# A two-layer decoder trunk (differential attention, then RWKV-7) on one NeuronCore: LoRA products begun with half of the tokens, states ahead of T's rows, T's loads between the masks

## The chip, the cores and the metric

The kernel runs on one core of one Trainium2 chip. The metric is the device time of one execution in microseconds, the median of several runs. TensorE multiplies matrices (PE in the profile, PEld for its weight loads), VectorE (DVE), ScalarE (ACT) and GpSimd (POOL) work element by element, SyncE (SP) issues most DMAs. Each engine takes its instructions in the order in which the program lists them for that engine.

## The reference

The trunk has two residual layers on 512 tokens of width 2048, all in float32. The first is gated differential attention, the second gated RWKV-7 time mixing:

```python
def rwkv7_mixer(h, ...):
    p = h @ w_in                                  # r, k, v, gate: 4 x 2048; dw, da: 96 each
    p = p + (token_shift(p) - p) * mu
    w_log = -softplus(-(w0 + tanh(dw) @ decay_up)) - 0.5
    decay = exp(-exp(w_log))
    a = sigmoid(a0 + da @ iclr_up)
    kk = heads(k * k_k);  kk = kk / max(norm(kk), 1e-12)
    k = k * (1.0 + (a - 1.0) * k_a)
    y = wkv7_scan(rh, heads(decay), kh, vh, -kk, kk * ah)   # S <- S*w + (S a) b' + v k';  y = S r
    y = group_norm(y) + sum(rh * kh * r_k) * vh
    return (y * silu(g)) @ w_out

for i in range(2):
    x = x + mixer_i(rms_norm(x, norm_w[i]))
```

There are 32 heads of 64 channels in the second layer; the scan runs over 512 tokens with a 64 x 64 state for each head.

## The kernel before

**Products.** Every large product is made of three matmuls on a high and a low part of both factors (`mm3`, L110 to 118), 16 channel tiles k of 128 for one sum. A weight is loaded on SP's queue (`wraw`), its high part is cast on ACT (`wh`, L102), its low part is the difference on DVE (`wl`, L103). Activations are split in the same way: `hH` on ACT, `hL` on DVE.

**Chains and ticks.** Work of another pair of heads runs between the matmuls of a projection. A `Chain` is a generator of steps, each of which yields the number of matmuls until the next. Every matmul of `mm3` that has the context counts as a tick of the oldest chain (`tick`); when its count is up, the next step is issued behind that matmul. If that step left a state (`g.state`), one item of `g.later`, elementwise work of the next pair, is issued behind it. What is still in `g.later` is issued by `stage2`. Priorities (`AHEAD`, `SCAN`, `SOLVE`) let a scheduler put instructions earlier in an engine's order; a larger one goes first.

**Between the layers.** The last columns of the first layer's output projection leave x, 4 blocks of 512 columns by 4 tiles of 128 tokens, in `xs`. `store_x` writes such a tile to memory and sums its squares (`junkx`, L727). The second layer's RMS norm then needs a reciprocal root for two token tiles at a time and a multiplication of each x tile by it (`scale`, L770): tokens 0 to 255 first, 256 to 511 last. `more_h` (L782 to 797) transposes a channel tile of all four token tiles into one PSUM bank (`xT`, L790) and splits it with `make_h` (L811, 812). The first products of the second layer are the LoRA down projections of decay and learning rate (192 columns in two sums of 96, `lora`), through `unit_chan` with `more_h`.

**The second layer's loop** goes over 16 pairs of heads, j. A pair's stages are spread over several rounds. Round j does, on PE: `stage2(j)` (makes `AR`, L1005, from the receptances), the V projection of j, `begin(j+1)` (K projection, and `stage1`, which puts `decays`, `queries`, `keys` of j+1 into `g.later`), the gate projection of j − 2 and the R projection of j + 1. Behind the 18th matmul of the V projection the function `behind` ends the chain of j − 2, issues `gram(j)`, `t_solve(j)` and `group_norm(j − 2)`.

- `gram` multiplies keys by queries in chunks of 64 tokens into PSUM (`gp`, L1021; first half with tag "pb", second half with tag "pc", two buffers each). With j > 1 it takes one step of the chain of j − 1 behind that. Then ACT copies to `G`, POOL writes the parts that T needs to memory (`ltd`) and masks G of head 0 and of head 1 (L1046, L1048).
- `t_solve` loads them again as `LT` (POOL's queue, L1071), inverts the triangles T row by row on DVE (`tmpl` L1082, `Tm` L1084, 31 rows; last L1085), and writes them to memory (`td`, L1086).
- The chain of j (`t_combine`, then `scan_pair`) loads `TT` from `td` on SP's queue (L1098), transposes it on DVE (`T1`, in the trace `T<-TT`, L1106), waits GAP_D ticks, multiplies with G (`px`, L1112), copies the result to `X` and a row of queries (`AR`) into G on ACT, waits GAP_X ticks, multiplies by TT (`px`, L1122). Then come eight chunks of the scan: `sm` (L1193) to `rhs`, `sm` (L1204) to `VS`, `sm` (L1211) to the next state `VS` on DVE (L1215, L1218), with copies of the state on POOL (`SA`, L1199) that are scaled by the decay (`Sg`, L1202). At the end `outputs` writes `Y` (L1233, L1237) into two PSUM banks of tag "pc", and `centre` subtracts the heads' means on DVE (`yc`, L1248 to 1250).
- `group_norm`, `finish_y` and `gated` make the rows of `yd2` in memory.

**The end.** After the loop the gates of the last pairs are projected; `gated(..., True)` splits the last two rows into high and low parts, `split_rows` the earlier ones as they come back from memory (`hH<-yr`, L421), and the output projection follows.

Of the kernel before, what the change touches and what calls it, by code (L numbers as in the profile page):

```python
# [13 lines left out]
F32 = mybir.dt.float32  # L14
# [4 lines left out]
ALU = mybir.AluOpType  # L19
# [16 lines left out]
    pass  # L36


AHEAD, SCAN, SOLVE = 2000, 3000, 4000


def ahead(offset):
# [549 lines left out]
def layer0(g, aps):  # L592
# [86 lines left out]
    with ExitStack() as cx:  # L679
# [42 lines left out]

        def store_x(cb, t):
            xr = xs[cb][:, t, :]
            nc.scalar.dma_start(out=g.xd[t * P : (t + 1) * P, cb * 512 : cb * 512 + 512], in_=xr)
            junk = g.work.tile([P, 512], F32, name="junkx", tag="a", bufs=2)
            nc.scalar.activation(junk[:], xr, AF.Square, accum_out=g.ssx[:, t, cb : cb + 1])  # L727

        sums = []
        one = lambda *tags: [(g.const if t[:2] == "dd" else g.work, t,  # L730
# [51 lines left out]
        def more_h(n, m):  # L782
            for k in range(len(g.hH), min(n, KT)):
# [7 lines left out]
                with tc.high_priority(offset=AHEAD):  # L791
                    make_h(g, ps, KT + k)

        pts = [g.ps.tile([P, 512], F32, name="lora", tag=tag) for tag in ("pb", "pc")]
        unit_chan(g, [(aps["rw_w_in"][0], 4 * D, 2 * RK)], 2 * RK, RK, more_h, pts=pts)
        g.dwda = []
        for i in range(2):
            m = shift_mix(g, pts[i], RK, g.mut[:, i : i + 1], g.omut[:, i : i + 1], "t1", 4)
# [3 lines left out]
    lx.close()  # L802


def make_h(g, ps, col):

    nc = g.nc
    hh = g.hp.tile([P, T], F32R, name="hH", tag="hH")
    hl = g.hp.tile([P, T], F32R, name="hL", tag="hL")
    w = g.prm_a[:, col : col + 1]  # L810
    m = nc.scalar.activation(hh[:], ps[:], AF.Copy, scale=w)  # L811
    d = nc.vector.scalar_tensor_tensor(hl[:], ps[:], w, hh[:].bitcast(F32), ALU.mult, ALU.subtract)
    g.hH.append(hh)
    g.hL.append(hl)
    return m.ins, d.ins


# [126 lines left out]
def stage1(g, j, k, up):  # L944
# [24 lines left out]
    def decays():  # L969
        nc.vector.tensor_tensor_scan(l[:].rearrange("p c t -> p (c t)"), g.rmask[:].rearrange("p c t -> p (c t)"),  # L970
                                     lw[:], 0.0, ALU.mult, ALU.add)
        nc.vector.tensor_scalar(m[:], l[:, :, C - 1], 0.5, None, ALU.mult)
        nc.vector.tensor_sub(l[:], l[:], m[:, :, None].to_broadcast([P, NC_, C]))
        nc.scalar.activation(p.E[:, :, 0], m[:], AF.Exp, scale=-1.0)
        nc.scalar.activation(p.E[:, :, 1:], l[:], AF.Exp)
        nc.scalar.activation(l[:], l[:], AF.Exp, scale=-1.0)
        nc.scalar.activation(p.f[:], tha[:], AF.Identity, bias=col("omka"), scale=col("hka"))
# [14 lines left out]
        nc.vector.tensor_add(p.gam[:, 0 : NC_ - 1], m[:, 0 : NC_ - 1], m[:, 1:NC_])  # L992
        nc.scalar.activation(p.gam[:, 0 : NC_ - 1], p.gam[:, 0 : NC_ - 1], AF.Exp)

    g.later += [decays, queries, keys]
    return p


# [11 lines left out]
def gram(g, j, p, before):  # L1010
# [30 lines left out]
                out=g.ltd[j % 2, half, h, :, 0:HALF].rearrange("c s t -> s c t"),  # L1041
                in_=p.G[q0 : q0 + HALF, :, 0, h, half * HALF : (half + 1) * HALF])

    for h in range(2):
        r_ = slice(h * C, h * C + C)
        nc.gpsimd.affine_select(out=p.G[r_, :, 0, 1 - h, :], in_=p.G[r_, :, 0, 1 - h, :], compare_op=ALU.is_ge,  # L1046
                                fill=0.0, base=-1, pattern=[[0, NC_], [1, C]], channel_multiplier=-1)
        nc.gpsimd.affine_select(out=p.G[r_, :, 1], in_=p.G[r_, :, 1], compare_op=ALU.is_ge, fill=0.0, base=0,  # L1048
                                pattern=[[0, NC_], [0, 2], [1, C]], channel_multiplier=-1)
# [11 lines left out]
@ahead(SOLVE)  # L1061
def t_solve(g, j, p):


    nc, w = g.nc, g.work
    NQ = HALF // NG
    LT = w.tile([P, HALF + 1, HALF], F32, name="LT", tag="LT", bufs=1)
    Tm = w.tile([P, NQ, HALF], F32, name="Tm", tag="Tm", bufs=1)
    tmp = w.tile([P, NQ * HALF], F32, name="tmpl", tag="tmpl", bufs=1)
    for i in range(NG):  # L1070
        nc.gpsimd.dma_start(out=LT[i * 32 : i * 32 + 32], in_=g.ltd[j % 2].rearrange("b h c s t -> (b h c) s t"))  # L1071
    n2 = LT[:, HALF, :]
    nc.vector.tensor_scalar(n2, n2, 1e-24, None, ALU.max)
# [11 lines left out]
    nc.vector.tensor_mul(Tm[:], Tm[:], n2[:, None, :].to_broadcast([P, NQ, HALF]))  # L1085
    nc.gpsimd.dma_start(out=g.td[j % 2].rearrange("q l t -> l q t"), in_=Tm[:])  # L1086


GAP_D, GAP_X, GAP_T = 18, 19, 8


def t_combine(g, j, p):
# [58 lines left out]
            nc.scalar.copy(p.VS[(1 - h) * C : (2 - h) * C, par : NC_ : 2, h, :], pv[par * C : par * C + C, :, h, :])  # L1151


def gate(g, j, gps):
    nc, w = g.nc, g.work
    gt = shift_mix(g, gps, P, *mus(g, 3, j), "v", 1)
    th = w.tile([P, T], F32, name="thg", tag="thg", bufs=1)
    nc.scalar.activation(th[:], gt[:], AF.Tanh, scale=0.5)
    nc.vector.scalar_tensor_tensor(gt[:], th[:], 1.0, gt[:], ALU.add, ALU.mult)
    return gt  # L1160


def gated(g, j, p, gt, last=False):
    g.nc.vector.tensor_mul(gt[:], gt[:], p.y[:])
    if last:
        return split_row(g, gt[:])
    g.nc.scalar.dma_start(out=g.yd2[j * P : (j + 1) * P, :], in_=gt[:])


# [12 lines left out]
def scan_pair(g, j, p, gap, gap_s, others):  # L1182
# [8 lines left out]
    for c in range(NC_):  # L1191
# [19 lines left out]
        nc.tensor.matmul(sm[:, o : o + P], p.BKT[:, c, :], both(VS[:, c]), start=True, stop=True)  # L1211
        for h, r_ in HEADS:
            s_ = sm[r_, o + h * C : o + h * C + C]
            if c:
                g.state = nc.vector.scalar_tensor_tensor(VS[r_, c + 1, h, :], s_, p.gam[r_, c : c + 1], Sg[r_, :],  # L1215
                                                         ALU.mult, ALU.add)
            else:
                nc.vector.tensor_scalar(VS[r_, c + 1, h, :], s_, p.gam[r_, c : c + 1], None, ALU.mult)  # L1218
        if c in others:
            others[c]()  # L1220
        yield gap_s
# [54 lines left out]
def layer1(g, aps):  # L1276
    nc, tc = g.nc, g.tc
    with ExitStack() as cx:
# [23 lines left out]
        for j in range(D // P):  # L1302
# [13 lines left out]
            def behind(m, j=j, p=p):  # L1316
                if j > 1:
                    pairs[j - 2].chain.finish(g)
                with tc.issue_after(m.ins):
                    gram(g, j, p, j > 1 and pairs[j - 1].chain)  # L1320
                t_solve(g, j, p)
                if j > 1:
                    group_norm(g, j - 2, pairs[j - 2])

# [131 lines left out]
```

## Time and profile before

| | us |
|---|---|
| median of 3 runs (lowest, highest) | 2209.49 (2206.18, 2210.26) |
| profiled execution, its own time | 2213.33 |
| its span | 2211.6 |
| PE busy | 2173.2 |
| DVE busy | 1445.7 |
| ACT busy | 1040.9 |
| POOL busy | 359.8 |

The span is the time from the profile's first instruction to its last. Times are us from its start, unless marked ns. In the views, a row gives engine, line, operation and tile names, `out<-in`; a bracket at the end gives how long the engine stood idle before the instruction and what it waited for. The granted clock is 1.00 at full speed. The first layer ends at 978.3 us, the loop over the pairs runs to about 2026 us, and the rest is the output projection.

### The profile page before, as it was taken

How to read it: one execution, taken by the hardware profiler on the slowest of the kernel's cores; microseconds unless marked ns; L12 is line 12 of the kernel's file. 1: busy time of each engine (PE TensorE's matmuls, PEld its weight loads, DVE VectorE, ACT ScalarE, POOL GpSimd, SP SyncE). 2: the span in 40 equal slices, each digit the busy share in tenths (PEclk: the TensorE clock that was granted, in tenths of full speed). 3: DMA queues.
4: the chain of work that ended last, by engine and by line, in shares of the span. 5: the costliest groups of instructions: out<-in, count | busy, mean ns of one | idle time of the engine just before them, and what ended most of it. 6: DMA issues, size and time to landing. Idle time of an engine off the chain costs nothing. (4 is left out here: it accounts for less than half of the span.)

```text
span 2211.6 us, 33922 instructions
## 1 busy us (share of the span) xinstructions
PE 2173.2 (98%) x12202; PEld 1762.5 (80%) x12202; DVE 1445.7 (65%) x3772; ACT 1040.9 (47%) x2110; POOL 359.8 (16%) x733
## 2 busy tenths in 40 slices
PE   9999999999999999989999999999999999999999
PEld 7888888888888878867777777778777777777887
DVE  5664646455564666465677788677777777777645
ACT  6443434344343454335455555555555556545322
POOL 0000000000000000110233233333332233331001
PEclk9999999999999999999999999999999999999999
DMA  6322232222222356643422333333333332345456
GB/s 192 97 85 97 77 102 89 87 95 86 96 86 95 129 183 213 162 106 90 106 67 78 79 92 86 82 91 94 98 91 82 89 88 75 107 131 182 174 166 120
DMA packets 281401, 240.21 MB, mean 109 GB/s; under 512 B 31792, under 2 KB 239744, under 8 KB 281232
## 3 DMA queue, kind: packets, MB, share of 16 engines
q1 hardware_dynamic: 256912, 190.13, 28.5%
q0 software_dynamic: 15456, 31.90, 6.7%
q10 hardware_dynamic: 8864, 16.01, 2.0%
q8 instruction: 96, 1.57, 0.3%
q14 instruction: 73, 0.60, 0.1%
HBM read 217.98 MB, written 19.99 MB: 108 GB/s over the span
## 5 line engine op out<-in xcount | busy, mean ns | idle before, releaser
L103 DVE TENSOR_TENSOR wl<-wraw,wh 128x1024 fp32r<-128x1024 f32 (+2 forms) x319 | 388.8, 1219 | 360.9 <-ACT wh L102 353.9
L102 ACT CAST wh<-wraw 128x1024 fp32r<-128x1024 f32 (+2 forms) x319 | 333.4, 1045 | 535.3 <-PE pp L114 374.5
L114 PE MATMUL pp<-wh,hH 128*128 128x512 f32 x1268 | 499.8, 394 | 4.0 <-ACT hH L421 2.4
L114 PE MATMUL pp<-wl,hH 128*128 128x512 f32 x1268 | 498.0, 393 | 0.0
L114 PE MATMUL pp<-wh,hL 128*128 128x512 f32 x1268 | 497.7, 393 | 0.0
L114 PE MATMUL pp<-hL,wh 128*128 128x512 f32 x1024 | 417.6, 408 | 0.0
L114 PE MATMUL pp<-hH,wl 128*128 128x512 f32 x1024 | 417.1, 407 | 0.0
L114 PE MATMUL pp<-hH,wh 128*128 128x512 f32 x1024 | 412.1, 402 | 0.0
L114 PEld LDWEIGHTS pp<-wh,hH 128*128 128x128 f32 x1268 | 238.6, 188 | 52.9 <-ACT hH L421 2.8
L114 PEld LDWEIGHTS pp<-wh,hL 128*128 128x128 f32 x1268 | 238.5, 188 | 47.9
L114 PEld LDWEIGHTS pp<-wl,hH 128*128 128x128 f32 x1268 | 238.8, 188 | 46.7
L114 PEld LDWEIGHTS pp<-hH,wh 128*128 128x128 f32 x1024 | 195.1, 191 | 37.0 <-issue 1.2
L114 PEld LDWEIGHTS pp<-hL,wh 128*128 128x128 f32 x1024 | 194.8, 190 | 35.2
L114 PEld LDWEIGHTS pp<-hH,wl 128*128 128x128 f32 x1024 | 195.0, 190 | 31.4
L1082 DVE SCALAR_TENSOR_TENSOR tmpl<-LT,Tm 128x60 f32<-128x60 f32 (+24 forms) x496 | 133.1, 268 | 10.6
L459 POOL DMA_DIRECT2D frow<-yd x12 | 8.9, 739 | 796.4 <-DVE rs_i L63 676.6
L1199 POOL COPY SA<-VS 64x64 f32<-64x64 f32 x224 | 61.2, 273 | 428.2 <-DVE VS L1215 382.9
L1084 DVE TENSOR_TENSOR Tm<-Tm,tmpl 128x60 f32<-128x60 f32 (+24 forms) x496 | 104.2, 210 | 11.2
L1215 DVE SCALAR_TENSOR_TENSOR VS<-sm,gam,Sg 64x64 f32<-64x64 f32 x192 | 54.2, 282 | 50.9 <-PE sm L1211 46.5
L1196 ACT COPY rhs<-sm 64x64 f32<-64x64 f32 x256 | 52.8, 206 | 63.6 <-PE sm L1193 61.1
L1206 ACT COPY VS<-sm 64x64 f32<-64x64 f32 x256 | 52.8, 206 | 62.0 <-PE sm L1204 58.3
L1202 POOL TENSOR_SCALAR Sg<-SA,gam 128x64 f32<-128x64 f32 x96 | 72.9, 759 | 9.3
(326 smaller groups left out, 3224.0 us busy)
## 6 DMA issues: line engine op xcount, KB each, us to landing
wraw<-in_rw_w_in_dram SPq DMA_DIRECT2D x128, 512.0 KB, 3.8
wraw<-in_da_w_in_dram SPq DMA_DIRECT2D x254, 256.0 KB, 2.9
wraw<-in_da_w_out_dram SPq DMA_DIRECT2D x26, 512.0 KB, 4.4
wraw<-in_rw_w_out_dram SPq DMA_DIRECT2D x26, 512.0 KB, 3.9
LT<-ltd POOLq DMA_DIRECT2D x64, 132.0 KB, 2.9
yr<-yd SPq DMA_DIRECT2D x28, 256.0 KB, 3.5
frow<-yd POOLq DMA_DIRECT2D x12, 512.0 KB, 6.9
xq<-in_x_dram SPq DMA_DIRECT2D x16, 256.0 KB, 5.7
```

The lines of the kernel that those rows point to most:

```text
L102: nc.scalar.copy(hi[:, ks], raw[:, ks])
L103: nc.vector.tensor_sub(lo[:, ks], raw[:, ks], hi[:, ks].bitcast(F32))
L114: m = nc.tensor.matmul(out, a, b, start=s, stop=e, skip_group_check=skip)
L459: nc.gpsimd.dma_start(out=r, in_=src[k0 * P : (k0 + KG) * P, :].rearrange("(k p) t -> p k t", p=P))
L1082: nc.vector.scalar_tensor_tensor(tt, LT[:, i : i + 1, i + 1 :].to_broadcast([P, s, n]), n2[:, i : i + 1], Tm[:, 0:s, i : i + 1].to_broadca ...
L1084: nc.vector.tensor_add(Tm[:, 0:s, i + 1 :], Tm[:, 0:s, i + 1 :], tt)
L1196: nc.scalar.copy(rhs[r_, :], sm[r_, h * C : h * C + C])
L1199: nc.gpsimd.tensor_copy(p.SA[r_, c - 1, :], VS[r_, c, h, :])
L1202: nc.gpsimd.tensor_scalar(Sg[:], p.SA[:, c - 1, :], p.gam[:, c : c + 1], None, ALU.mult)
L1206: nc.scalar.copy(VS[r_, c, h, :], sm[r_, P : P + C])
L1215: g.state = nc.vector.scalar_tensor_tensor(VS[r_, c + 1, h, :], s_, p.gam[r_, c : c + 1], Sg[r_, :], ALU.mult, ALU.add)
```

## The change

It has these parts:

- LoRA products: `half_h` and `products` take the first eight channel tiles in two halves of 256 tokens each, the first half of all eight first; one PSUM bank holds the transposes of two channel tiles. The other eight follow as before. `make_h` can fill half of a tile. The squares in `store_x` go ahead of the DMA on ACT, with a higher priority for the last two column blocks.
- States: the scan's new states (L1215, L1218) are issued with priority STATE, above the rows of T.
- `exps`: the exponentials are cut from `decays` and made an item of their own in `g.later`, so `queries` and `keys` also come an item later.
- Masks: `mask_gram` is cut from `gram`; the masks of head 0 come before T's loads, those of head 1 behind them.
- `GAP_D` is 20 instead of 18. With it the step that `gram` takes runs the first `px` behind `gp`. Before, the first `px` was due just before `gp`, and that step ran the second.
- The end: the last two rows are split inside the output projection (`all_rows`), the split of the earlier rows no longer waits for the last but one, and the gate of the last pair uses the buffer of tag "E".

```diff
-AHEAD, SCAN, SOLVE = 2000, 3000, 4000
+AHEAD, SCAN, SOLVE, STATE = 2000, 3000, 4000, 8000
...
         def store_x(cb, t):
             xr = xs[cb][:, t, :]
+            junk = g.work.tile([P, 512], F32, name="junkx", tag="a", bufs=2)
+            with tc.high_priority(offset=SCAN if cb > 1 else 0):
+                nc.scalar.activation(junk[:], xr, AF.Square, accum_out=g.ssx[:, t, cb : cb + 1])
             nc.scalar.dma_start(out=g.xd[t * P : (t + 1) * P, cb * 512 : cb * 512 + 512], in_=xr)
-            junk = g.work.tile([P, 512], F32, name="junkx", tag="a", bufs=2)
-            nc.scalar.activation(junk[:], xr, AF.Square, accum_out=g.ssx[:, t, cb : cb + 1])
...
+        def half_h(k, half, m):
+            ps = g.ps.tile([P, 512], F32, name="xT", tag="pa", bufs=2)
+            for i in range(2):
+                xq, c0 = xs[(k + i) // 4], (k + i) % 4 * P
+                for t in range(2):
+                    tt, at = 2 * half + t, (2 * i + t) * P
+                    if c0 == 0 and half:
+                        scale((k + i) // 4, tt)
+                    with tc.issue_after(m.ins) if m else ExitStack():
+                        nc.tensor.transpose(ps[:, at : at + P], xq[:, tt, c0 : c0 + P], g.ident[:])
+            for i in range(2):
+                with tc.high_priority(offset=AHEAD):
+                    make_h(g, ps[:, 256 * i : 256 * i + 256], KT + k + i, k + i, half)
...
-        unit_chan(g, [(aps["rw_w_in"][0], 4 * D, 2 * RK)], 2 * RK, RK, more_h, pts=pts)
+        lora = [(aps["rw_w_in"][0], 4 * D, 2 * RK)]
+        def products(k, wt, s, m):
+            for c in range(2):
+                wh, wl = [x[:, k % 4, c * RK : (c + 1) * RK] for x in wt]
+                m = mm3(nc, pts[c][:RK, s], wh, wl, g.hH[k][:, s], g.hL[k][:, s],
+                        k == 0 and s.start == 0, k == KT - 1, g, True)
+            return m
+        m, wts = None, []
+        turns = [(k, half) for half in range(2) for k in range(0, KT // 2, 2)]
+        for i, (k, half) in enumerate(turns):
+            if i == 0:
+                half_h(k, half, m)
+            if i + 1 < len(turns):
+                half_h(*turns[i + 1], m)
+            else:
+                more_h(KT // 2 + 1, m)
+            if half == 0 and k % 4 == 0:
+                wts.append(split_w(g, lora, 4, 2 * RK, k))
+            for kk in (k, k + 1):
+                m = products(kk, wts[kk // 4], slice(256 * half, 256 * half + 256), m)
+        for k in range(KT // 2, KT):
+            if k % 4 == 0:
+                wts.append(split_w(g, lora, 4, 2 * RK, k))
+            more_h(k + 2, m)
+            m = products(k, wts[k // 4], slice(0, T), m)
...
+    def exps():
         nc.scalar.activation(p.E[:, :, 0], m[:], AF.Exp, scale=-1.0)
...
-    g.later += [decays, queries, keys]
+    g.later += [decays, exps, queries, keys]
...
-    for h in range(2):
-        r_ = slice(h * C, h * C + C)
+def mask_gram(g, p, h):
+    nc = g.nc
+    for r_ in [slice(h * C, h * C + C)]:
         nc.gpsimd.affine_select(out=p.G[r_, :, 0, 1 - h, :], in_=p.G[r_, :, 0, 1 - h, :], compare_op=ALU.is_ge,
...
-GAP_D, GAP_X, GAP_T = 18, 19, 8
+GAP_D, GAP_X, GAP_T = 20, 19, 8
...
-def gate(g, j, gps):
+def gate(g, j, gps, tag="v"):
...
     if last:
-        return split_row(g, gt[:])
+        return
...
-            if c:
-                g.state = nc.vector.scalar_tensor_tensor(VS[r_, c + 1, h, :], s_, p.gam[r_, c : c + 1], Sg[r_, :],
-                                                         ALU.mult, ALU.add)
-            else:
-                nc.vector.tensor_scalar(VS[r_, c + 1, h, :], s_, p.gam[r_, c : c + 1], None, ALU.mult)
+            with g.tc.high_priority(offset=STATE):
+                if c:
+                    g.state = nc.vector.scalar_tensor_tensor(VS[r_, c + 1, h, :], s_, p.gam[r_, c : c + 1], Sg[r_, :],
+                                                             ALU.mult, ALU.add)
+                else:
+                    nc.vector.tensor_scalar(VS[r_, c + 1, h, :], s_, p.gam[r_, c : c + 1], None, ALU.mult)
...
-                t_solve(g, j, p)
+                mask_gram(g, p, 0)
+                loaded = t_solve(g, j, p)
+                with tc.issue_after(loaded):
+                    mask_gram(g, p, 1)
...
-        gt = gate(g, j - 1, gps)
-        row = []
+        gts = [gate(g, j - 1, gps)]
...
-                row.append(gated(g, j - 1, pairs[j - 1], gt, True))
+                gated(g, j - 1, pairs[j - 1], gts[0], True)
...
-        gt = gate(g, j, proj(3, j, behind=(24, last_but_one)))
-        rows = split_rows(g, g.yd2, ("r", "k", "th0", "th1", "l", "f", "xH", "xL"), 1, j - 1) + row
+        gts.append(gate(g, j, proj(3, j, behind=(24, last_but_one)), "E"))
+        rows = split_rows(g, g.yd2, ("r", "k", "th0", "th1", "l", "f", "xH", "xL"), 1, j - 1)
 
         def all_rows(n, _):
+            if n >= 4 and len(rows) == KT - 2:
+                rows.append(split_row(g, gts[0][:]))
             if n >= KT and len(rows) < KT:
                 group_norm(g, j, p)
                 finish_y(g, j, p)
-                rows.append(gated(g, j, p, gt, True))
+                gated(g, j, p, gts[1], True)
+                rows.append(split_row(g, gts[1][:]))
```

More of the change, by code (lines that the diff above doesn't have):

```diff
@@ L802, in layer0, with make_h @@
     lx.close()
-def make_h(g, ps, col):
+def make_h(g, ps, col, k=None, half=None):
     nc = g.nc
-    hh = g.hp.tile([P, T], F32R, name="hH", tag="hH")
-    hl = g.hp.tile([P, T], F32R, name="hL", tag="hL")
+    if not half:
+        g.hH.append(g.hp.tile([P, T], F32R, name="hH", tag="hH"))
+        g.hL.append(g.hp.tile([P, T], F32R, name="hL", tag="hL"))
+    s = slice(0, T) if half is None else slice(256 * half, 256 * half + 256)
+    hh, hl = [x[-1 if k is None else k][:, s] for x in (g.hH, g.hL)]
     w = g.prm_a[:, col : col + 1]
[L811 to L814, printed above, removed]
+    m = nc.scalar.activation(hh, ps[:], AF.Copy, scale=w)
+    d = nc.vector.scalar_tensor_tensor(hl, ps[:], w, hh.bitcast(F32), ALU.mult, ALU.subtract)
     return m.ins, d.ins
@@ L1070, in t_solve @@
     for i in range(NG):
-        nc.gpsimd.dma_start(out=LT[i * 32 : i * 32 + 32], in_=g.ltd[j % 2].rearrange("b h c s t -> (b h c) s t"))
+        ld = nc.gpsimd.dma_start(out=LT[i * 32 : i * 32 + 32], in_=g.ltd[j % 2].rearrange("b h c s t -> (b h c) s t"))
     n2 = LT[:, HALF, :]
@@ L1086, in t_solve @@
     nc.gpsimd.dma_start(out=g.td[j % 2].rearrange("q l t -> l q t"), in_=Tm[:])
-GAP_D, GAP_X, GAP_T = 18, 19, 8
+    return ld.ins
+GAP_D, GAP_X, GAP_T = 20, 19, 8
 def t_combine(g, j, p):
@@ L1151, in turn_values @@
             nc.scalar.copy(p.VS[(1 - h) * C : (2 - h) * C, par : NC_ : 2, h, :], pv[par * C : par * C + C, :, h, :])
-def gate(g, j, gps):
+def gate(g, j, gps, tag="v"):
     nc, w = g.nc, g.work
-    gt = shift_mix(g, gps, P, *mus(g, 3, j), "v", 1)
+    gt = shift_mix(g, gps, P, *mus(g, 3, j), tag, 1)
     th = w.tile([P, T], F32, name="thg", tag="thg", bufs=1)
```

## The prediction

> **What bounds the kernel now.** I read the engines' busy times first, then TensorE's waits, then windows in which its clock falls.
>
> ```profile
> PE 2173.2 (98%) x12202; PEld 1762.5 (80%) x12202; DVE 1445.7 (65%) x3772; ACT 1040.9 (47%) x2110; POOL 359.8 (16%) x733
> ```
>
> TensorE (PE) is busy for 2173.2 of 2211.6 us. The change removes no product, so what it can win lies in 38.4 us of gaps and in matmuls that run at a lowered clock. The waits (who waited, for what: us in total, times, longest):
>
> ```profile
> PE px L1112 <- DVE T L1106: 7.4, 10, 2.4
> PE xT L790 <- DVE xq L770: 5.0, 1, 5.0
> PE sm L1193 <- DVE VS L1215: 3.6, 15, 0.5
> PE pp L114 <- ACT hH L421: 2.4, 1, 2.4
> PE gp L1021 <- DVE AR L1005: 1.1, 1, 1.1
> ```
>
> Each of these rows has a part of the change aimed at it. The windows below have the columns us, busy time of PE, weight loads, DVE, ACT, POOL, then granted clock, DMA share, GB/s:
>
> ```profile
> 981.70:988.60 6.90, 3.58 (x10) 2.13 (x11) 6.34 (x23) 1.27 (x2) 0.00 (x0) 0.51 0.10 33
> 1097.80:1111.40 13.60, 13.43 (x88) 10.49 (x89) 3.02 (x5) 5.23 (x12) 3.17 (x5) 0.50 0.32 81
> 1387.90:1391.30 3.40, 2.66 (x50) 2.15 (x50) 2.95 (x5) 1.57 (x4) 0.00 (x0) 1.00 0.68 171
> 1391.30:1398.20 6.90, 6.90 (x61) 5.63 (x58) 0.69 (x1) 4.65 (x10) 2.64 (x5) 0.51 0.09 13
> 2029.60:2033.00 3.40, 3.40 (x11) 2.75 (x10) 2.68 (x5) 3.36 (x9) 0.00 (x0) 0.50 0.68 219
> ```
>
> After a stall the clock falls to about .50 for one to four windows of 3.4 us, and in the second layer PE, busy all through, does half its work there: 6.8, 3.4 and 1.7 us lost in the stretches at 1097.80, 1391.30 and 2029.60, 11.9 together. So a stall's price is its idle time and, in some cases, 1.7 us or a multiple.
>
> The Trainium skill, page "TensorE: Matmul & The Clock Gate", section "HAM oscillation — how this bites in real kernels", gives as the abstract rule that idle gaps over about 3.4 us cool the clock. By it gaps under 2.5 us cost only their idle time, and the 11.9 us would stay. The trace differs: in 1387.90 to 1391.30 PE was busy for 2.66 of 3.40 us, and the clock still fell to .51. The measurement decides; the rule's result is the fourth rival.
>
> In the second layer, gp (the gram products) follows gp at a fixed place in each pair of heads. From the chain that ended last:
>
> ```profile
> 1327.41 1.99 PE gp L1021 x32
> ...
> 1578.44 1.99 PE gp L1021 x32
> 1640.81 2.06 PE gp L1021 x32
> ...
> 1893.28 2.06 PE gp L1021 x32
> ```
>
> Nine periods take 1893.28 − 1327.41 = 565.9 us, 62.87 each. What sets a period is a ring around T:
>
> ```profile
> 1597.59 0.18 DVE L1073 TENSOR_SCALAR LT<-LT 128x32 f32<-128x32 f32 x1
> ...
> 1631.40 0.42 DVE L1085 TENSOR_TENSOR Tm<-Tm,LT 128x256 f32<-128x256 f32 x1
> 1631.91 0.76 DVE L1248 TENSOR_REDUCE s<-Y 128x4 f32<-128x256 f32 x2
> 1632.78 0.75 DVE L1250 TENSOR_TENSOR yc<-Y,s 128x256 f32<-128x256 f32 x2
> ...
> 1638.30 0.44 DVE L1106 STREAM_TRANSPOSE T<-TT 64x256 f32<-64x256 f32 x1 [1.04 <-DMA TT<-td]
> ...
> 1639.59 0.44 DVE L1106 STREAM_TRANSPOSE T<-TT 64x256 f32<-64x256 f32 x1 [0.22 <-DMA TT<-td]
> ```
> ```profile
> 1640.09 0.69 PE L1112 MATMUL px<-T,G 32*32 32x32 f32 x16 [0.26 <-DVE T L1106]
> ```
>
> gp at 1578.44; solve from 1597.59 (19.15 later) to 1631.82 (34.23); then td out, TT back, the second transpose done at 1640.03 (8.21); px; next gp at 1640.81 (.78). The sum is 62.37. So a period shrinks only as far as this ring does.
>
> **The change part by part.**
>
> LoRA products. Here before:
>
> ```profile
> 979.25 0.44 PE L790 MATMUL xT<-ident,xq 128*128 128x128 f32 x2 [0.24 <-DVE xq L523]
> 984.66 1.30 PE L790 MATMUL xT<-ident,xq 128*128 128x128 f32 x4 [4.97 <-DVE xq L770]
> ...
> 990.62 0.60 PE L790 MATMUL xT<-ident,xq 128*128 128x128 f32 x4
> ...
> 992.45 0.38 PE L790 MATMUL xT<-ident,xq 128*128 128x128 f32 x2
> ```
> ```profile
> 979.87 0.61 ACT L727 ACTIVATE junkx<-xq 128x512 f32<-128x512 f32 x1
> ```
> ```profile
> 981.57 0.15 DVE L774 TENSOR_REDUCE ss<-ssx 128x2 f32<-128x8 f32 x1
> ...
> 983.92 0.16 DVE L70 SCALAR_TENSOR_TENSOR rs<-rs_t,rs_i 128x2 f32<-128x2 f32 x1
> 984.12 2.07 DVE L770 TENSOR_SCALAR xq<-xq,rs 128x512 f32<-128x512 f32 x5
> 986.30 1.41 DVE L812 SCALAR_TENSOR_TENSOR hL<-xT,prmin_norm_w_dram,hH 128x512 fp32r<-128x512 f32 x2
> ```
>
> PE waits 4.97 us for the scales of the second half of the tokens, though the first half is ready at 979.25. Afterwards one channel tile takes 992.45 − 990.62 = 1.83 us. In the changed order PE begins on half 0, but not at once: hH stands on ACT behind the squares (to 980.5), and each hL of half a tile (about .35, half of 1.41/2) alternates on DVE with 13 small operations at about .2 (981.57 to 984.08) and eight scales of .41 (2.07/5): 2.5 + 3.3 = 5.8 us. I estimate about 1 us per half tile to 989.6, so some eight halves, four tiles; before, (989.6 − 985.5)/1.83 = 2.2 tiles were done. (4 − 2.2) × 1.83 = 3.3 us won. It cannot exceed the wait and half the slow window, 5.0 + 3.4, less the 1.6 from 979.25 to a first hH at 980.9, so 6.8; at worst the halves crawl at the scales' pace and it wins 1. The 48 products that become 96 of half width cost little, by starts in the trace:
>
> ```profile
> 837.00 0.28 PE L114 MATMUL o<-V,al 128*128 128x256 f32 x1
> 837.11 0.39 PE L114 MATMUL pp<-wh,hH 128*128 128x512 f32 x1
> 837.35 0.40 PE L114 MATMUL pp<-wl,hH 128*128 128x512 f32 x1
> ```
>
> a start follows a 256-wide one by .11 and a 512-wide one by .24, so 96 × .11 − 48 × .24 is −1 to 0 with the rounding; I count 0. The squares put ahead of the DMA that stores x on ACT's queue delay that store by .6 each; the program reads it again only in the last projection.
>
> The steady loop, eleven pairs. New order on PE: Y is finished in the V projection, gp runs and px's first products follow it instead of standing around it; the second px comes 19 matmuls later. T's deadline therefore moves behind gp. But gp's second half writes a PSUM buffer that Y held, so it waits for yc, and on DVE, which keeps its order, yc's last piece stands behind both transposes, which wait for TT. The ring after goes by these rows of POOL and DVE:
>
> ```profile
> 1587.91 0.66 POOL L1046 TENSOR_SCALAR_AFFINE_SELECT G<-G 64x512 f32<-64x512 f32 x1
> ...
> 1589.63 1.99 POOL L1071 DMA_DIRECT2D LT<-ltd  x4
> ```
> ```profile
> 1600.55 0.28 DVE L1215 SCALAR_TENSOR_TENSOR VS<-sm,gam,Sg 64x64 f32<-64x64 f32 x1 [0.76 <-PE sm L1211]
> ...
> 1640.79 0.75 DVE L1006 SCALAR_TENSOR_TENSOR mixr<-mixr,prm_hrk,f 128x512 f32<-128x512 f32 x1
> ```
>
> From gp to the end of Tm: LT's loads go out on POOL ahead of two of the four masks, 1589.63 − 1587.91 = 1.7 earlier, less about 1 because one copy of G now stands on ACT behind X, which waits for px. The masks move behind the loads and end at 1591.6 instead of 1589.6; POOL's next work, copies of the state, starts behind them in either order, so nothing waits for that. T's rows, however, then stand behind state 1 on DVE and begin some 2 us after 1597.59, my estimate. Little is done in those 2 us now, and state 1 (.28 for a head, with .76 of idle before it) no longer stands between the rows. State 6 now stands ahead of the last rows (0 to .6). So gp to the end of Tm stays 19.15 + 34.23 = 53.4, bounds 52.5 to 54.0.
>
> From Tm to the last transpose: 8.2 now, td's way unchanged (SP issues TT's loads at the same place). Between the transposes now stand a sum of Y, a yc piece (half of .76 and of .75) and the product at L1006: 1.5 at most, of which the time from the first transpose to the second now (1639.59 − 1638.30 − .44 = .85) covers a part: +.6. Then .4 of yc, and gp's second half starts 1.03 after its first: −.65 in place of +.78.
>
> 53.4 + 8.8 − .65 = 61.6, against 62.37 in this pair and 62.87 on average, where the half-clock windows are. Winning all of 62.87 − 61.6 = 1.3 would need every window gone; I take .75, since some waits stay and move to gp: 11 × .75 = 8.3. Bounds: the ring at its best 60.7, −24; or 64.5, with T late and a slow window most times, +18. Putting states first can win at most their wait, 3.6; it does not shorten the ring, so I count nothing for it. The exponentials, a state later on ACT, with queries and keys behind them, are hidden by the receptance projection; without that cover gp waits for AR, as it did once for 1.1.
>
> The first pairs have no Y in front of gp, and there px follows the same counts as before. Pair 0's stall
>
> ```profile
> 1097.97 0.74 PE L1112 MATMUL px<-T,G 32*32 32x32 f32 x10 [2.41 <-DVE T L1106]
> ```
>
> and the 6.8 lost behind it hang on a solve that begins when DVE has split a weight, not on LT. Loads 1.8 earlier relieve that weight's transfer at best. Of 2.4 + 6.8 I take a third: −3 (−8 to +1).
>
> The tail. Rows of yd2 are cast early, under the last projection, and row 14 only between products, so the 2.4 at 2029.1 and the 1.7 behind it go: −3.5. The eleven casts stand on ACT ahead of X, which holds the last pair's second px back:
>
> ```profile
> 2028.48 1.65 ACT L421 CAST hH<-yr 128x512 fp32r<-128x512 f32 x3
> ```
>
> 11 × .55 = 6.0, against 16 products of .24 between the two px, 3.8: at worst 2.2 of waiting, if all rows land at once. Bounds −4.1 and −1.3.
>
> Sum: −3.3 − 8.3 − 3 − 3.5 = −18.1. Against the profiled execution's own 2213.33 us that is 2195.2. This execution lay 3.8 above the median of the runs, 2209.49, and the result will be a median, so I forecast **2191.5**.
>
> **The rivals.**
>
> *The wait only moves.* px waits less and gp's second half waits as much, behind yc. For it: the ring's terms are the same DMAs, which make up most of 8.21 us. Against it: the deadline that is 1.4 later (.78 + .65). The loop and the first pairs give nothing: 2209.5 − 6.8 = 2202.7, own range 2197 to 2212.
>
> *T late: slower.* T's last rows stand behind states 1 to 6, which wait on PE, ACT and POOL; place: gp's second half, in every pair. Today the slack is nil: px waited .26 in the pair shown. If the solve ends 2 us later than I have it, the period is 61.6 + 2 and, since PE idles 2 us in one window, 1.7 of lost clock follows: 65.3, 2.4 more than 62.87. 11 × 2.4 = 27, less 6.8: 2230, own range 2214 to 2243. It decides once gp's second half waits over 1.1 us on average. For it: state 1 ahead of everything begins the solve later. Against: DVE is idle or does other work (weights, decays) in those places already.
>
> *Everything goes.* All stalls in the loop and the slow windows: 2177.
>
> *The clock does not follow these stalls,* as in the skill's rule: the slow windows stay, and only idle is won: px's 5 us in the loop, 3 to 5 elsewhere, 2.4 in the tail, so 11: 2198.5. The window at 1097.80 of four periods after one stall speaks a little for it, that each slow stretch begins behind a stall against it.
>
> That the change does nothing is excluded for the tail and the LoRA part, by the order on the queues.
>
> **How the numbers follow.** Forecast .40 (own range 2182 to 2203), wait moves .26, T late .22, everything .08, clock .04. Below 0.2% (4.4 us) the measurement cannot tell from no change; the borders are 2205.1 and 2213.9. Faster: .40 + .11 (of the second) + .08 + .04 = .63. Same: .15 of the second. Slower: .22. Range 2178 to 2227: it leaves out half of "everything" and the upper half of "T late", under 2 in 10.
>
> **What would show it.** Right: no wait of 5 us at the transposes ahead of the LoRA products and some four tiles done by 989.6; px without waits at L1162 from the third pair on; gp to gp near 61.6; no stall at the hH cast near the end, fewer windows at .50. Wrong: gp waiting for yc by more than 1 us in most pairs, Tm ending more than 54 after gp, the ring unchanged at 62.9, or ACT's row casts holding back the last X by more than 2 us.

## The result, and the profile after

The changed kernel takes 2221.11 us (median of 6 runs, 2219.97 to 2228.30), the kernel before in the same comparison 2206.93 (6 runs, 2205.59 to 2210.26): a ratio of 1.0067, 95% interval 1.0052 to 1.0082. The change makes the kernel slower by two thirds of a per cent. The profiled execution of the changed kernel is its longest run, 2228.3 us with a span of 2226.4; that of the kernel before took 2213.33, so the two lie 7.2 and 6.4 above their medians.

Where the time went shows best when both spans are cut at the same events. The table holds differences of times in the two traces (gp n is the start of the first gram product of pair n, L1021 before and L1067 after; the LoRA products and the last product are taken at their end):

| stretch, us | before | after | difference | forecast |
|---|---|---|---|---|
| start to the last product of the first layer | 978.08 | 981.42 | +3.3 | 0 |
| from there to the end of the LoRA products | 38.42 | 35.16 | −3.3 | −3.3 |
| to gp 0 | 26.98 | 26.96 | 0 | 0 |
| gp 0 to gp 4 | 221.43 | 218.73 | −2.7 | −3 |
| gp 4 to gp 15, eleven pairs | 690.08 | 706.10 | +16.0 | −8.3 |
| gp 15 to the last product | 252.47 | 253.91 | +1.4 | −3.5 |

The first row is no part of the change: 3.0 of the 3.3 us are there at the 21st product (it starts at 16.74 instead of 13.76), long before anything that was changed, and in the other kernels of this study the row's point lies anywhere from 978.1 to 983.1. The loop over the steady pairs is where the forecast fails: a period of 63.9 us instead of 62.8. The 16.0 are those of one execution: e3 below, whose median is that of the changed kernel within .4 us, has 698.7 in that row of its profile.

TensorE's waits in that loop (who waited, for what: us in total, times, longest) hold three that are new or grown. First the one on T before, then after:

```profile
PE px L1112 <- DVE T L1106: 2.8, 7, 0.6
```
```profile
PE sm L1254 <- ACT rhs L1246: 8.7, 20, 1.7
PE gp L1067 <- DVE yc L1301: 7.9, 8, 1.2
PE sm L1243 <- DVE VS L1266: 3.8, 8, 0.5
```

px's wait for T is gone from the loop, but gp now waits for yc. How this comes about is seen around one gp of the changed kernel. First DVE, then PE (start us, us, engine, line, operation):

```profile
1643.06 0.69 DVE L1051 TENSOR_TENSOR AR<-mixr,E 128x512 f32<-128x512 f32 x1
1643.67 0.42 DVE L1299 TENSOR_REDUCE s<-Y 128x4 f32<-128x256 f32 x1
1645.60 0.44 DVE L1156 STREAM_TRANSPOSE T<-TT 64x256 f32<-64x256 f32 x1 [1.51 <-DMA TT<-td]
...
1646.34 0.40 DVE L1301 TENSOR_TENSOR yc<-Y,s 128x256 f32<-128x256 f32 x1
...
1646.74 0.74 DVE L1052 SCALAR_TENSOR_TENSOR mixr<-mixr,prm_hrk,f 128x512 f32<-128x512 f32 x1
1647.51 0.44 DVE L1156 STREAM_TRANSPOSE T<-TT 64x256 f32<-64x256 f32 x1
1647.98 0.42 DVE L1301 TENSOR_TENSOR yc<-Y,s 128x256 f32<-128x256 f32 x1
```
```profile
1646.37 1.38 PE L1067 MATMUL gp<-AR,BK 64*128 64x128 f32 x18
1648.55 1.13 PE L1067 MATMUL gp<-AR,BK 64*128 64x128 f32 x14 [0.80 <-DVE yc L1301]
1649.61 1.09 PE L1162 MATMUL px<-T,G 32*32 32x32 f32 x32
```

Y's first sum is ready by 1644.1, but the transpose of T stands next on DVE and waits 1.51 us for TT. Both pieces of yc come behind it, the second behind the other transpose as well, and gp's second half waits for that. So gp, which needs nothing of T, starts its second half when T is there.

The second link is on ACT and POOL, behind the same gp:

```profile
1649.53 0.58 ACT L1074 COPY G<-gp 128x512 f32<-128x512 f32 x1 [0.89 <-PE gp L1067]
1650.33 0.62 ACT L1168 COPY G<-AR 64x512 f32<-64x512 f32 x1 [0.22 <-PE px L1162]
1650.96 0.74 ACT L1165 COPY X<-px 32x256 f32<-32x256 f32 x2
1651.72 0.62 ACT L1168 COPY G<-AR 64x512 f32<-64x512 f32 x1
1652.37 0.59 ACT L1074 COPY G<-gp 128x512 f32<-128x512 f32 x1
1652.98 1.05 ACT L102 CAST wh<-wraw 128x1024 fp32r<-128x1024 f32 x1
1653.93 0.57 ACT L1078 COPY ssl<-pt 2x512 f32<-2x512 f32 x1
```
```profile
1654.79 1.14 POOL L1080 DMA_DIRECT2D ltd<-ssl  x2 [0.39 <-ACT ssl L1078]
1655.99 0.65 POOL L1095 TENSOR_SCALAR_AFFINE_SELECT G<-G 64x512 f32<-64x512 f32 x1
1656.61 1.15 POOL L1097 TENSOR_SCALAR_AFFINE_SELECT G<-G 64x1024 f32<-64x1024 f32 x1
1659.67 0.52 POOL L1120 DMA_DIRECT2D LT<-ltd  x1 [1.91 <-DMA ltd<-ssl]
```

The norms of the keys (ssl) stand on ACT behind X, so behind px, so behind T. Their write to memory is now the last that T's loads wait for: POOL stands idle for 1.91 us at the loads, with two masks ahead of them instead of four. In the kernel before, ssl was copied earlier, the masks filled that time, and the loads went out without a wait:

```profile
1582.79 0.58 ACT L1032 COPY ssl<-pt 2x512 f32<-2x512 f32 x1
```
```profile
1588.53 1.16 POOL L1048 TENSOR_SCALAR_AFFINE_SELECT G<-G 64x1024 f32<-64x1024 f32 x1
1589.63 0.52 POOL L1071 DMA_DIRECT2D LT<-ltd  x1
```

The ring of the prediction, in means over the ten pairs 4 to 13, all from starts, ends and landings in the traces ("landed": the last of the four transfers of LT has arrived). The last four columns are experiments that follow:

| us, mean of ten pairs | before | after | GAP_D alone (e1) | all but GAP_D (e2) | yc ahead (e4) | px later (e8) |
|---|---|---|---|---|---|---|
| gp, start to end | 2.20 | 3.28 | 2.95 | 2.11 | 2.05 | 2.05 |
| gp's end to ssl on ACT | 2.30 | 4.43 | 4.26 | 2.19 | 4.26 | 1.05 |
| gp's end to LT landed | 13.88 | 14.67 | 14.44 | 13.13 | 14.38 | 11.61 |
| gp's end to Tm's end | 51.72 | 53.47 | 51.95 | 49.64 | 53.21 | 49.93 |
| gp's start to the second T transposed | 62.04 | 65.58 | 63.41 | 61.24 | 63.02 | 62.68 |
| period, gp to gp | 62.84 | 63.91 | 62.72 | 62.96 | 62.43 | 62.21 |

### The profile page after: what moved, and what is told of

It reads as the page before. It is cut to its first block, busy times and chain, and to the rows that moved or that the text cites. A ratio compares the mean times of both kernels' runs of the same rounds, so it can differ in the third digit from the quotient of the medians.

```text
span 2226.4 us, 34057 instructions
## 1 busy us (share of the span) xinstructions
PE 2178.6 (98%) x12250; PEld 1772.0 (80%) x12250; DVE 1447.4 (65%) x3780; ACT 1046.3 (47%) x2118; POOL 345.6 (16%) x733
## 5 line engine op out<-in xcount | busy, mean ns | idle before, releaser
L114 PEld LDWEIGHTS pp<-hH,wh 128*128 128x128 f32 x1024 | 194.9, 190 | 34.9 <-issue 1.7
L114 PEld LDWEIGHTS pp<-hL,wh 128*128 128x128 f32 x1024 | 194.8, 190 | 34.8
L1074 ACT COPY G<-gp 128x512 f32<-128x512 f32 x64 | 35.0, 591 | 93.5 <-PE gp L1067 93.1
L1254 PEld LDWEIGHTS sm<-rhs,TT 128*128 128x128 f32 x256 | 45.2, 189 | 34.9 <-ACT rhs L1246 26.8
```

What stands on the lines that cost most here:

```text
L114: m = nc.tensor.matmul(out, a, b, start=s, stop=e, skip_group_check=skip)
L1074: nc.scalar.copy(p.G[:, c0 : c0 + 4, :, h, :], gp[h][:].rearrange("p (u x t) -> p u x t", u=4, x=2))
L1254: nc.tensor.matmul(sm[:, P : P + C], both(g.TT[j % 2][:, c]), rhs[:], start=True, stop=True)
```

## The experiments

All were timed in five rounds beside the kernel before; ratios are to that kernel, with 95% intervals. "The loop" is 1320 to 1960 us.

Three theories stood at first. A: the new order around gp, which `GAP_D` makes, is the loss. B and C: the exponentials an item later hold up ACT, or the states ahead of T's rows lengthen the solve.

**e1, GAP_D alone**, on the kernel before:

```diff
-GAP_D, GAP_X, GAP_T = 18, 19, 8
+GAP_D, GAP_X, GAP_T = 20, 19, 8
```

> The kernel before with GAP_D = 20 alone. Theory A (the loss comes from the order that GAP_D makes around gp: Y only 13 products ahead of gp, yc behind T's transposes on DVE, the fourth copy of G behind X on ACT): slower than before by 8 to 16 us, gp to gp about 64 us from the fourth pair on, gp waiting for yc near 1 us in most pairs. Theory B (exponentials a state later hold up ACT, so that sm waits for rhs: 8.7 us of the loop in the changed kernel) and theory C (states ahead of T's rows lengthen the solve, 35.5 us against 34.8): no change, within 4 us of before, no wait of gp for yc of weight.

Measured: 2209.97 us, ratio 1.0006 (0.9995 to 1.0017). The order of PE is that of the changed kernel, gp waits 2.4 us in the loop, and the time is that of the kernel before. Theory A as stated falls, though `GAP_D` is not quite free: e1's runs were granted a slightly higher clock, which hides some 3 us of waits (estimated behind e12).

**e2, all but GAP_D**, on the changed kernel:

```diff
-GAP_D, GAP_X, GAP_T = 20, 19, 8
+GAP_D, GAP_X, GAP_T = 18, 19, 8
```

> The changed kernel with GAP_D = 18. Theory A: faster than before by 2 to 8 us (the LoRA part and the tail stay), gp to gp 62 to 62.9, no wait of gp for yc. Theories B and C: still slower than before by 8 us or more, with the waits of sm for rhs (B) or a solve of 35.5 us (C) in the trace.

Measured: 2202.35 us, 0.9974 (0.9957 to 0.9991). The part from gp 15 to the end takes 246.0 us, 6.4 less than before. Its loop from gp 4 to gp 15 takes 691.7 us, 1.6 more than before. So B and C fall too, as the cause of the loss: neither GAP_D nor the rest costs much alone. Only together do they lose, and the difference between e2 and the changed kernel, .93%, is the price of the two products more of GAP_D in this company. T's loads land 13.1 us after gp's end, .75 earlier than before, which fits what the masks' split is for; the rows had promised 1.7.

**e3, the copies of gp first on ACT**, on the changed kernel:

```diff
     for c0, gp in halves:
         for h in range(2):
-            nc.scalar.copy(p.G[:, c0 : c0 + 4, :, h, :], ...)
+            with g.tc.high_priority(offset=STATE):
+                nc.scalar.copy(p.G[:, c0 : c0 + 4, :, h, :], ...)
```

> The changed kernel, the four copies of gp to G ahead of X and of the queries' copies on ACT. Theory A: T's loads land 1.5 to 2.5 us earlier after gp's end, gp to gp falls from 63.9 to 62 or 62.5, the time from 2221 to 2202 to 2210. If the fourth copy is not on the ring (B, C): 2217 to 2224.

Measured: 2220.72 us, 1.0064 (1.0048 to 1.0080), LT landed 14.7 after gp's end, as without the edit. The fourth copy now starts .3 after gp's end instead of 2.7, but ssl still comes behind X, at 4.2, and its write lands at 9.55 as before the edit (9.53). The row of POOL at the loads, here for the same pair, says the same:

```profile
1656.31 2.01 POOL L1121 DMA_DIRECT2D LT<-ltd  x4 [2.69 <-DMA ltd<-ssl]
```

I had picked the wrong copy: the one that counts is that of the norms.

**e4, T's transposes behind yc**, on the changed kernel. The transposes move from `t_combine`'s first step into its second:

```diff
-    for h in range(2):
-        r_ = slice(h * C, h * C + C)
-        nc.vector.transpose(T1[r_], TT[r_, :, h, 0:HALF])
     yield GAP_D
+    with g.tc.issue_after(g.centred.ins) if g.centred else ExitStack():
+        for h in range(2):
+            r_ = slice(h * C, h * C + C)
+            nc.vector.transpose(T1[r_], TT[r_, :, h, 0:HALF])
...
-        nc.vector.tensor_sub(p.yc[:, h::2, :], ...)
+        g.centred = nc.vector.tensor_sub(p.yc[:, h::2, :], ...)
```

> The changed kernel with T's two transposes ordered behind yc on DVE, so that gp does not wait for T any more. Theory A: px stands right behind gp, so the wait moves from gp (8.3 us) to px, and the fourth copy of G still stands behind X, which comes out of px: the ring is as long, 2217 to 2224. A rival (the wait of gp for yc is the price, and nothing else): the 8.3 us go, 2210 to 2215.

Measured: 2206.76 us, 0.9995 (0.9985 to 1.0005), .72% less than the changed kernel. The waits in the loop have no row of gp and none of px:

```profile
PE sm L1255 <- ACT rhs L1247: 6.8, 19, 0.4
PE sm L1244 <- DVE VS L1267: 5.1, 10, 0.5
PE sm L1262 <- ACT VS L1257: 0.2, 1, 0.2
```

T is transposed 63.0 after the gp before, px comes 64.4 after it. The expectation that the wait would pass to px was wrong, and so was the rival's size. The order of DVE behind Y is the loss against the kernel before: without it the two times agree (e2 is still .21% faster). T itself is hardly late; but one transpose that waits holds yc, gp and everything behind gp. The norms are as late here as in the changed kernel (ssl 4.26 after gp's end, as in e1), so their lateness alone does not make the loss; what it costs by itself was not measured.

A new theory, D: GAP_D = 20 puts T's transposes, yc and gp's second half in series. That is nearly free while T is early (e1); the other parts make T some 1.5 us later (Tm's end 53.5 after gp's end, 52.0 with GAP_D alone), and then every pair pays. E: the exponentials alone do it.

**e5, e6, e7: one part of the changed kernel undone each.** e5, the states at their old priority:

```diff
-            with g.tc.high_priority(offset=STATE):
-                if c:
+            if c:
```

> The changed kernel with the states at their old priority. Theory D (GAP_D = 20 puts T's transposes, yc and gp's second half in series, which costs nothing while T is early, as with GAP_D alone; the states ahead of T's rows and the work put among them make T late, Tm ends 53.5 us after gp's end against 52.0 with GAP_D alone; only both together cost): Tm ends 52.0 to 52.6 after gp's end, gp waits for yc under 4 us in the loop, gp to gp 62.5 to 63.0, time 2203 to 2212. Theory E (the exponentials an item later do it): 2216 to 2224, Tm still 53.3 to 53.6 after gp's end.

Measured: 2214.14 us, 1.0012 (1.0001 to 1.0024): .55% less than the changed kernel, the largest of the three, and between the ranges of the two theories. gp's waits for yc are gone; Tm ends 49.8 after gp's end, earlier than either theory had it. Part of that is given back in another place:

```profile
PE sm L1243 <- DVE VS L1265: 4.6, 10, 0.5
PE gp L1067 <- DVE AR L1051: 4.2, 3, 2.7
PE sm L1254 <- ACT rhs L1246: 4.2, 11, 1.6
```

In this kernel's order both transposes stand ahead of AR on DVE, and the first of them waits 2.9 to 6.0 us for TT in every pair; where it waits longest, 5.95 us ahead of the gp at 1642.59, gp waits 2.7 us for AR behind it. The kernel differs in that order too, so this is not the states' price alone.

e6, the exponentials in the decays' item:

```diff
-    def exps():
...
-    g.later += [decays, exps, queries, keys]
+    g.later += [decays, queries, keys]
```

> The changed kernel with the exponentials in the decays' item again. Theory E: sm waits for rhs 4 to 5 us in the loop instead of 8.7, Tm ends 52.0 to 52.6 after gp's end, 2203 to 2212. Theory D: 2216 to 2224, with gp's wait for yc still near 8 us.

Measured: 2218.91 us, 1.0034 (1.0021 to 1.0047). sm waits 3.4 us for rhs in the loop instead of 8.7, as E said; gp still waits 6.1 for yc and Tm ends 53.3 after gp's end, as D said. Both costs exist, but the exponentials' place is not the only source of waits for rhs: e1, which has it as before, shows 4.3 us of them.

e7, all masks ahead of the loads:

```diff
-                mask_gram(g, p, 0)
-                loaded = t_solve(g, j, p)
-                with tc.issue_after(loaded):
-                    mask_gram(g, p, 1)
+                t_solve(g, j, p)
```

> The changed kernel with all four masks ahead of T's loads again. Both theories: T's loads land within .5 us of the changed kernel's, 14.7 after gp's end (GAP_D alone had 14.4), 2217 to 2224. If the masks' place counts: loads 1.7 later, 2225 to 2240.

Measured: 2219.90 us, 1.0044 (1.0032 to 1.0056). T's loads land at 14.7 after gp's end, unmoved: the split gains nothing here, since the loads wait for ssl. The interval touches that of the changed kernel, so whether the split costs anything stays open.

**e9, three parts and nothing else**: the kernel before with GAP_D = 20, the states ahead and the exponentials an item later:

```diff
-GAP_D, GAP_X, GAP_T = 18, 19, 8
+GAP_D, GAP_X, GAP_T = 20, 19, 8
...
+            with g.tc.high_priority(offset=STATE):
...
-    g.later += [decays, queries, keys]
+    g.later += [decays, exps, queries, keys]
```

> The kernel before with GAP_D = 20, the states ahead and the exponentials an item later, and nothing else of the change. Theory D (each alone is cheap, together they make T late in a series that has no room): gp to gp 63.2 to 64, gp waits for yc 5 to 9 us in the loop, Tm ends 53 to 53.6 after gp's end, 8 to 16 us slower than before. If the LoRA part, the masks or the tail are needed for the loss: within 4 us of before.

Measured: 2225.50 us, 1.0064 (1.0041 to 1.0087). Tm ends 53.4 after gp's end, the period is 63.8, and the waits in the loop are those of the changed kernel:

```profile
PE gp L1023 <- DVE yc L1253: 8.2, 15, 1.0
PE sm L1206 <- ACT rhs L1198: 5.8, 20, 0.4
PE sm L1213 <- ACT VS L1208: 2.4, 13, 0.2
```

D holds in this: these three are enough for the loss; GAP_D without the others (e1) and the others without GAP_D (e2) are not. How the states and the exponentials share it is not settled, since e5 has another order on DVE as well.

**e8, px six products behind gp**, on e3 and e4 together. The transposes get a step of their own and px comes later, so that ssl and all copies of G precede X on ACT; the second px follows sooner, and Y stays where it was:

```diff
-GAP_D, GAP_X, GAP_T = 20, 19, 8
+GAP_D, GAP_P, GAP_X, GAP_T = 20, 6, 13, 8
...
             nc.vector.transpose(T1[r_], TT[r_, :, h, 0:HALF])
+    yield GAP_P
```

> The changed kernel with T's transposes behind yc, the first px six products after gp, the second 13 products later, and the copies of G ahead of the rest on ACT. Theory D: T has 1.5 us more room, gp waits for nothing, the loop goes at PE's pace: gp to gp 61.5 to 62.4, 2196 to 2206. If T's lateness isn't the limit (the waits of sm for rhs and state are): 62.4 as with yc ahead alone, 2204 to 2209.

Measured: 2199.77 us, 0.9952 (0.9940 to 0.9963). Around the gp of the same pair, on ACT and POOL:

```profile
1631.86 2.05 ACT L1075 COPY G<-gp 128x512 f32<-128x512 f32 x4 [5.40 <-PE gp L1067]
1633.77 0.57 ACT L1079 COPY ssl<-pt 2x512 f32<-2x512 f32 x1
...
1635.83 0.74 ACT L1168 COPY X<-px 32x256 f32<-32x256 f32 x2
```
```profile
1637.89 1.15 POOL L1098 TENSOR_SCALAR_AFFINE_SELECT G<-G 64x1024 f32<-64x1024 f32 x1
1639.18 1.04 POOL L1121 DMA_DIRECT2D LT<-ltd  x2
```

ssl follows the copies of G at once, the loads go out without the wait of 1.91 for ssl, and LT lands 11.6 after gp's end instead of 14.7. T is now transposed 3.5 us ahead of px. No half-clock window is left in the loop. What remains there are 8.0 us of sm waiting for rhs.

**e10, e8 with the exponentials in the decays' item**:

```diff
-    def exps():
...
-    g.later += [decays, exps, queries, keys]
+    g.later += [decays, queries, keys]
```

> As e8, with the exponentials in the decays' item. In e8 gp waits for nothing and what is left in the loop are 8.0 us in which sm waits for rhs on ACT. Theory E2 (these waits come from the exponentials' place): 3 to 5 us of them left, gp to gp 61.8 to 62.0, 2 to 5 us faster than e8. If ACT holds rhs back for other reasons: within 2 us of e8.

Measured: 2194.32 us, 0.9921 (0.9901 to 0.9941), gp to gp 61.63, sm's waits for rhs 3.8 us. E2 holds, though the intervals of e8 and e10 just touch and gp to gp fell a little more than expected. Where T has room, the exponentials' place costs .58 us a pair on ACT.

**e11, e8 with the last pair's chain begun earlier**:

```diff
-        chain(g, j, p, 66, 5, 6)
+        chain(g, j, p, 46, 5, 6)
```

> As e8, with the last pair's chain begun 20 products earlier (46 instead of 66). In e8 its T was ready 7.8 us ahead of px, and the part from the last gp to the end took 251 us against 246 with GAP_D = 18. If the late chain in the tail is what costs there: 247 to 248.5 us, 2.5 to 4 us faster than e8. If not: within 1.5 us of e8.

Measured: 2197.99 us, 0.9937 (0.9916 to 0.9957); gp 15 to the end 248.1 us instead of 251.2, which is the 3 us expected in that stretch. The whole time moved by 1.8, and the intervals of e8 and e11 overlap.

**e12, e10 and e11 together**:

> e10 and e11 in one kernel, a candidate for the fastest: 2191 to 2197 if both gain, 0.5 to 0.8% under the kernel before.

Measured: 2189.39 us, 0.9904 (0.9882 to 0.9925): faster than both kernels of this case, 1.0% under the kernel before, and below the expected 2191. The edits are those of e8, e10 and e11, nothing else. From the chain that ended last, gp is as regular as PE's own work:

```profile
1450.37 1.99 PE gp L1065 x32
1511.99 1.99 PE gp L1065 x32
1573.61 1.99 PE gp L1065 x32
1635.23 1.99 PE gp L1065 x32
```

**What of this is the clock.** Each run has its mean granted clock, and its span times one minus that clock estimates what half-clock windows cost it, to about 1 us and as if PE were busy in all of them. In medians over the runs: 13.2 us in the kernel before as timed beside e1 to e8, 12.2 in the changed one, 11.0 in e1, 7.7 in e2, 5.5 in e8, 4.4 in e12. By this estimate the changed kernel does not lose by the clock; its 14 us are waits. GAP_D alone has 2.2 less of the clock at .8 more time, so some 3 us more of waits. And most of what e2 (6.8) and e8 (10.4) gain on the kernel before, 5.5 and 7.7 us, lies in windows that no longer fall.

## Why the prediction was wrong

The range (2178 to 2227) holds the time, the sign is wrong: forecast −0.8%, measured +0.67%. By its steps:

- **LoRA, −3.3: right in size.** The stretch shrinks by 3.26 us. The forecast's count of tiles was off on both sides: by 989.6 the kernel before had done 1.3 tiles and not 2.2, with PE at .50 until 988.57; at the same distance from the first layer's last product the changed one had done 3.4 and not four. PE no longer waits 4.97 us for the second half's scales; what it waits for are the casts and differences, as the prediction had it:

```profile
982.06 1.25 PE L805 MATMUL xT<-ident,xq 128*128 128x128 f32 x8 [0.25 <-DVE xq L523]
984.33 0.47 PE L114 MATMUL lora<-hH,wh 128*96 128x256 f32 x2 [1.01 <-ACT hH L857]
984.96 0.36 PE L114 MATMUL lora<-hL,wh 128*96 128x256 f32 x1 [0.15 <-DVE hL L858]
```

- **The first pairs, −3: right in size for this execution (−2.7), its reason not tested.** Pair 0's stall stayed (2.36 us against 2.41), as the prediction said of a solve that hangs on a weight. Kernels of this study with and without the masks' split range from 217.0 to 226.4 us in that stretch, with the half-clock windows that fall there, so the number proves little: these windows alone take 10.2 us where the kernel before had 17.1, and half of that difference is 3.4. The agreement is luck as far as this trace shows.

- **The steady loop, −8.3: wrong, +16.0.** The failing step is "So gp to the end of Tm stays 19.15 + 34.23 = 53.4, bounds 52.5 to 54.0". It is 56.75 on average, outside the bounds. The pair that the step was read from was a good one: the ten pairs' mean of the kernel before is 53.92, .5 more. Three terms of it were off, which against that mean are +1.08, +.79 and +.97. gp itself, which I let run on for 2.06 us, is 3.28 long, since its second half waits. The loads, "1.7 earlier, less about 1", land .8 later after gp's end, because I followed the fourth copy of G behind X and not the norms behind it, which come later still; the 1.91 us of POOL's idle shows it, and e8 takes it away. And from the landing to Tm's end pass 38.8 us where it were 37.8, though the forecast had the solve end no later: DVE comes to it later after the landing (3.9 us instead of 3.6), and from the first operation on LT to Tm's end it takes 34.9 us where it took 34.2 (the 35.5 and 34.8 in e1's expectation count DVE's wait just ahead of it too); undoing the states' priority (e5) brings that to 31.3 together with another order on DVE. The other two terms of the ring were right or better: Tm to the last transpose 8.8 (forecast 8.8), the deadline behind gp's start 1.67 (forecast .65). The ring as a way of counting held: 56.75 + 8.83 − 1.67 = 63.91. It was counted from gp's start with gp's length fixed, though gp's own wait is a part of it.

- **The rival "T late: slower" was the case, at half its price.** Its place (gp's second half, behind yc and T's transposes) and its point of decision (a wait of over 1.1 us on average) are what the trace shows: gp is 1.08 longer on average than before, and 1.22 longer than a gp without a wait. Its price of 2.4 a pair was too high, as the clock fell behind few of those waits: the loop has three half-clock windows, 10.2 us at .50, where the kernel before had 13.7. Its chance of .22 was too low. What spoke for it, state 1 ahead of the first rows, I had answered with DVE's idle places; e5 and e9 speak for this order as a part of the loss, though none of them has it by itself.

- **"The exponentials ... are hidden by the receptance projection": wrong in place.** They do not hold up AR. They stand on ACT ahead of rhs, in the scan: 8.7 us of waits, 3.4 of them left without the split (e6).

- **The tail, −3.5: wrong here, right without GAP_D.** The stall of 2.40 us at the cast is gone; one of .93 stands at a later cast. But GAP_D = 20 moves the last chain back as well, and PE stands still for a gate that DVE finishes late:

```profile
2043.46 0.50 PE L114 MATMUL pp<-wh,hH 128*128 128x512 f32 x1 [1.76 <-DVE mixE L898]
```

  A half-clock stretch of 6.8 us follows, 3.4 us lost. Without GAP_D (e2) the tail gains 6.4, more than the 4.1 that I had as a bound, and the wait for the gate is not there; with the last chain begun earlier (e11) it is gone too. But e1 and e9, which have GAP_D = 20 and the tail of the kernel before, have neither this wait nor the stall of 2.40, and take 249.5 and 249.4, 3 less than the kernel before. So with GAP_D = 20 the changed tail shows no gain of its own. I had priced the casts ahead of X at up to 2.2 and not the chain's own delay.

What stays open: why the solve takes 31.3 to 37.8 us in these kernels (e5 and e10), which is a matter of what DVE does between its rows, was not taken apart; nor was what the masks' split costs by itself, nor what the late norms do.

## What to carry to other kernels

Parts that are each free or nearly so can lose together: a new order is only as good as the slack of the chain that it puts in series, and another part may have used that slack up. Before moving a step next to another, list for each in-order engine what stands behind its result, not only the copy that is wanted but the last one that a load waits for. Where an instruction that waits for a transfer stands ahead of one that is ready, move the ready one ahead first; here that order alone was worth .7% of the kernel.

## What the runs showed of the hardware

The clock's answer to short stalls is not settled by their length. In the changed kernel, windows of the clock's own period (columns: us, busy time of PE, weight loads, DVE, ACT, POOL, then granted clock, DMA share, GB/s):

```profile
1454.40:1457.80 3.40, 2.42 (x50) 2.06 (x49) 0.99 (x3) 2.08 (x4) 0.35 (x1) 1.00 0.51 146
1457.83:1461.24 3.41, 3.41 (x9) 2.60 (x8) 0.00 (x0) 2.52 (x6) 1.76 (x4) 0.50 0.12 19
...
1836.70:1840.10 3.40, 2.20 (x25) 1.60 (x25) 2.74 (x8) 1.07 (x2) 0.00 (x0) 1.00 0.70 162
1840.10:1843.50 3.40, 3.40 (x53) 2.87 (x51) 0.00 (x0) 2.42 (x5) 1.18 (x2) 1.00 0.18 38
```

PE was busy for 2.42 us of the first window and the clock fell to .50 in the next; it was busy for 2.20 of the third and the clock stayed (both by matmul ends that the profile models). Of the gp waits between .8 and 1.2 us in the loop, two were followed by such a window and five were not. The Trainium skill, page "TensorE: Matmul & The Clock Gate", section "HAM oscillation — how this bites in real kernels", has the clock fall for idle gaps above about 3.4 us; no gap in this loop was longer than 1.7, so here the measurement differs from the page again. What decides between the two windows no run here shows.
